# Two mixing tiles become a seven-product pair, and the convolution streams are woven in earlier

## The chip, the cores and the metric

The kernel runs on one core of one Trainium2 chip. The metric is device time in microseconds of one execution; several executions are timed and their median is given. One execution was also profiled.

## The reference

One layer of a hybrid backbone is computed for two groups that share weights: 128 prompt tokens and 512 latent tokens (an 8 x 64 grid), width 1024, all in float32. Both groups are modulated and projected by the same `w_in`:

```python
h = x * (1 + scale) + shift
(v_h, x1, x0, g_h), (q, k, v, g_a), m = split_projection(h, p["w_in"], p["conv_w"], p["conv_b"])
y_h = hyena_long_conv(v_h, x1, x0, h_fwd, h_bwd, p["hyena_d"])   # ((u * filter) + u * d) * x0, u = v_h * x1
y_a = context_attention(q, k, v)              # prompt; latent tokens: neighbourhood_attention
p_h = (y_h * jax.nn.silu(g_h)) @ w_bh
p_a = (y_a * jax.nn.silu(g_a)) @ w_ba
m_h, m_a = jnp.split(jax.nn.sigmoid(m), 2, axis=-1)
out = (m_h * p_h + m_a * p_a) @ w_out
x_new = layer_norm(ALPHA * x + gate * out, p["ln_g"], p["ln_b"])
```

`v_h`, `x1` and `x0` pass a three-tap short convolution first (`split_projection`). The long convolution is done by Fourier transforms. The change concerns the mixing inputs `m` (1024 columns for `m_h`, 1024 for `m_a`) and the order of the work around the convolutions.

## The kernel before

Tokens of both groups stand together, 640 columns, channels on the 128 partitions. Every float32 number that goes into a large matmul is split in a high and a low part, and three products (high x high, high x low, low x high) are added. `hH` and `hL` are the two parts of the modulated input, eight blocks of 128 channels each. The columns of `w_in` are 80 tiles of 128 output channels.

There are two ways to compute projection tiles. `proj` does one tile: 8 blocks x 3 passes x 2 halves of 320 tokens, 48 matmuls of 128x128 by 128x320 (line 182). Its weights come by one load into `raw` on SyncE's queue (SP); ScalarE (ACT) writes the negative low start `wl`, an accumulating load on GpSimd's queue (POOL) adds the weights to it, and ACT writes the high part `wh` (`wtile`, lines 149 to 167). `pair_tile` does two tiles at once by a seven-product scheme on 2 x 2 blocks: seven products of 4 x 3 = 12 matmuls of the same size (line 1239), with sums of weight blocks and sums of token blocks as inputs. The token sums t1 to t4 are made early by `token_sums`, kept in DRAM (`tok_d`) and loaded again by `load_sums`; the weight sums are made by accumulating loads on POOL's queue (`blocks`) and by `sum1` and `sum6` on VectorE (DVE). `high` and `low` split each block sum, ACT the high part, DVE the low.

The program has these stages in order.

1. The prologue: modulation, first tiles, filter input layers.
2. The convolution phase. Its main generator is `quarters()`: per quarter of the channels, `quarter_head` (four short-convolution tiles for u = v_h * x1), `quarter_tail` (two tiles for x0) and a tile group of attention values. Woven into it, as the side generator, is `braid(convs(), filters())`: `long_conv` and `long_conv_back` for each quarter, and `filter_spectrum`, the filters' transforms. `weave(main, side, n_main, n_side)` advances the side n_side steps for each n_main steps of main; `AHEAD_OF` holds the two numbers. The order in which generators issue is a priority; the order on each engine is set from it by a planner when the program is built. `gate_conv(n)` multiplies x0 with the long convolution's output and stores it (`yu_d`), when the second of the two is there.
3. The hand-over (`hand_over`): last x0 tiles, values 0, queries 0, keys 0, then two mixing tiles by `mix_tile`, and the weight loads of the two tiles that follow. When the convolutions are through, `attention_setup` gives their memory to the attention.
4. From here to the end of the attention every engine's order is written out by hand. `first_gates` does two gate tiles by `proj` and prepares the first weight blocks. Then come the heads, eight pairs of attention heads j = 0 to 7, each with its list of pairs from `HEADS`: q makes queries and keys, h and a the branches' gates, m the mixing tiles. A pair counts 14 steps (half-products). The attention of head j (`attend`: scores `tiled`, transposes `turned`) is put between these steps, for j = 0 at the steps listed in line 1407. `later` and `tick` delay work by such steps.
5. The branch projections, the output projection and the norm.

Of the kernel before, what the change touches and what calls it, by code (L numbers as in the profile page):

```python
# [2 lines left out]

# [42 lines left out]
def tile_hyena_natten_step(ctx: ExitStack, tc: tile.TileContext, a, o):  # L46
# [404 lines left out]
        nc.scalar.activation(x[:, 4:10:5], two(pp[:]), AF.Copy)  # L451
        yield

    N_FILTER = 11

    zss = []
    for i in range(2):
# [68 lines left out]
    def quarter_tail(q):  # L526
        for i in range(2):
            n = 2 * q + i
            out["x0"][n] = row(yhp, "yh", f"x0_{n}", n=NG + 1)
            yield from conv_tile(16 + n, out["x0"][n])  # L530
            gate_conv(n)
            yield

    def long_conv(q):
        us, ident = out[f"u{q}"], out["ident"]
# [159 lines left out]

    N_VALUES = 11

    AHEAD_OF = 5, 3

    SUMS = ("t2", "t3", "t1", "t4")  # L700

# [50 lines left out]
    def chain(*gens):  # L752
        for g in gens:
            yield from g
# [4 lines left out]
    head = quarter_head(0)  # L759
    next(head)  # L760
    dft_consts()
    weave(head, filter_spectrum(0), 2 + NK, N_FILTER)
    pinned[0] = False
    sums = chain(token_sums(0), token_sums(1))

    def along(main, side, every):
        for i, _ in enumerate(main):
# [86 lines left out]
    def hand_over():  # L854
        yield from quarter_tail(3)
        hwa_stack.close()
        load_sums(0, SUMS[:2])
        out["slots_l"] = left.enter_context(tc.tile_pool(name="slots_l", bufs=1))
        out["slots_q"] = left.enter_context(tc.tile_pool(name="slots_q", bufs=1))
        first_blocks()  # L860
        yield from chain(values(0), queries(0), keys(0))
        yield from mix_tile(0)
        last_mix = mix_tile(1)
        yield next(last_mix)
        for i in range(2):
            wraw(T_GA + i)
        yield from last_mix
        for i in range(2):
            early[T_GA + i] = wtile(T_GA + i, "dma")
        load_a(0)  # L870

    def mix_tile(n):
        th = row(yhp, "yh", f"mx{n}")
        for hf, p in enumerate((yield from proj(T_MH + n, eng="dma"))):
            nc.scalar.activation(th[:, CS[hf]], p[:, :HALF], AF.Tanh, scale=0.5)
        nc.scalar.dma_start(mh_d[n], th[:])
        yield

    def first_gates():
        yield from gate_a(0)  # L880
# [510 lines left out]
    with tc.manual_schedule(engines=engines):  # L1391
        for _ in first_gates():
            pass
        sums_of_second()
        scratch()
        load_sums(0, SUMS[2:3])
        load_sums(1, SUMS[2:3])
        load_a(1)
        load_sums(0, SUMS[3:])
        load_sums(1, SUMS[3:])  # L1400
        biases[0] = [bias_tile(h) for h in range(2)]
        for j in range(8):
# [12 lines left out]
        drain()  # L1415
# [311 lines left out]
```

## Time and profile before

| | |
|---|---|
| median of three runs | 880.49 us (879.66 to 881.36) |
| the profiled execution | 881.71 us, span 879.9 us |
| TensorE (PE) busy | 867.0 us, 99% |
| VectorE (DVE) busy | 638.6 us, 73% |
| ScalarE (ACT) busy | 450.3 us, 51% |
| GpSimd (POOL) busy | 188.6 us, 21% |
| granted TensorE clock, mean | 0.997 |
| DMA | 169.09 MB, 192 GB/s over the span |

The span runs from the first to the last instruction; the execution's own time is 1.8 us more. In the profile's rows, a line such as L182 is the line of the kernel that issued the instruction, `out<-in` are tiles by name with buffer numbers left out, and an arrow in brackets names what ended the idle time before an instruction. PEld is the weight load of a matmul, which overlaps other matmuls.

### The profile page before, as it was taken

The numbers are of one execution on the slowest core, as the hardware profiler recorded it, in microseconds if no ns is written. First come the engines' busy times: TensorE is split into PE (matmuls) and PEld (weight loads), VectorE is DVE, ScalarE is ACT, GpSimd is POOL, SyncE is SP. The second block draws the span as 40 slices with busy tenths as digits, with TensorE's granted clock in tenths as the row PEclk, the third lists the DMA queues.
The fourth block names the chain that finished last, engine by engine and source line by source line (L and its number), as shares of the span: only waits on it lengthen the run. The fifth ranks groups of instructions, "written<-read, shape, count | busy, mean of one in ns | idle before, by whom it ended". The sixth has DMA issues, their size and how long they took to land.

```text
span 879.9 us, 17136 instructions
## 1 busy us (share of the span) xinstructions
PE 867.0 (99%) x6476; PEld 838.1 (95%) x6476; DVE 638.6 (73%) x1215; ACT 450.3 (51%) x956; POOL 188.6 (21%) x216
## 2 busy tenths in 40 slices
PE   8999999999999999999999999999999999999996
PEld 6899999999999999999999999999999999999885
DVE  4679896786786682588867787777777676666666
ACT  4396654545545535367565656656666622233200
POOL 0012211101101111147453434333453200000000
PEclk9999999999999999999999999999999999999998
DMA  8978876546656696998677668675854596445521
GB/s 311 402 175 232 226 212 150 139 108 169 144 119 146 161 224 143 332 299 230 182 214 187 196 163 251 142 219 162 226 143 113 189 337 206 164 151 187 188 91 53
DMA packets 75246, 169.09 MB, mean 192 GB/s; under 512 B 11003, under 2 KB 28667, under 8 KB 75164
## 3 DMA queue, kind: packets, MB, share of 16 engines
q1 hardware_dynamic: 56204, 123.06, 41.6%
q0 software_dynamic: 13632, 39.33, 23.2%
q10 hardware_dynamic: 5328, 5.61, 1.9%
q8 instruction: 51, 0.84, 0.4%
q14 instruction: 31, 0.25, 0.1%
HBM read 143.32 MB, written 23.99 MB: 190 GB/s over the span
## 4 chain that ended last, share of the span: by engine, by line
PE 96%; DVE 2%; ACT 1%; DMA 1%; issue 0%; POOL 0%; POOLq 0%; DVEq 0%; ACTq 0%
PE mm L182 36%; PE sp L1239 29%; PE out L1537 6%; PE v L661 5%; PE s L1045 2%; PE s L952 2%; PE pt L1036 2%; PE ve L672 1%; PE adaT L252 1%; DMA ra<-wall 1%; PE adaT L269 1%; PE fl L400 1%; PE yb L172 1%; PE yb L170 1%; PE yb L171 1%; PE fl L401 1%
## 5 line engine op out<-in xcount | busy, mean ns | idle before, releaser
L1239 PE MATMUL sp<-t,wb 128*128 128x320 f32 x1008 | 158.9, 311 | 0.0
L1239 PEld LDWEIGHTS sp<-t,wb 128*128 128x128 f32 x1008 | 150.1, 188 | 0.5 <-issue 0.5
L1239 PE MATMUL sp<-hH,wb 128*128 128x320 f32 x500 | 120.9, 313 | 0.0
L1239 PEld LDWEIGHTS sp<-hH,wb 128*128 128x128 f32 x500 | 86.0, 188 | 2.6 <-issue 2.6
L162 POOL DMA_DIRECT2D wl<-wall x34 | 30.4, 894 | 258.3 <-ACT wl L161 230.6
L182 PE MATMUL mm<-hH,wh 128*128 128x320 f32 x336 | 81.7, 313 | 0.7 <-ACT hH L328 0.5
L182 PE MATMUL mm<-hL,wh 128*128 128x320 f32 x336 | 80.8, 311 | 0.0
L182 PE MATMUL mm<-hH,wl 128*128 128x320 f32 x336 | 80.4, 310 | 0.4 <-DVE wl L102 0.4
L1239 PE MATMUL sp<-hL,wb 128*128 128x320 f32 x250 | 77.3, 309 | 0.0
L163 ACT ACTIVATE wh<-raw 128x1024 fp32r<-128x1024 f32 x34 | 36.1, 1062 | 48.8 <-PE mm L182 35.5
L1200 DVE TENSOR_TENSOR wb<-s,wb 128x512 fp32r<-128x512 f32 x63 | 45.0, 715 | 19.1 <-ACT wb L1192 18.9
L182 PEld LDWEIGHTS mm<-hH,wh 128*128 128x128 f32 x336 | 56.9, 188 | 1.9 <-ACT hH L328 0.8
L182 PEld LDWEIGHTS mm<-hH,wl 128*128 128x128 f32 x336 | 57.0, 188 | 1.1 <-DVE wl L102 0.9
L182 PEld LDWEIGHTS mm<-hL,wh 128*128 128x128 f32 x336 | 57.0, 188 | 0.9 <-DVE hL L329 0.5
L1007 POOL TENSOR_SCALAR edge<-edge,sm 128x320 f32<-128x320 f32 x32 | 43.3, 1511 | 61.7 <-DVE sm L1005 53.6
L1192 ACT ACTIVATE wb<-s 128x512 fp32r<-128x512 f32 x63 | 39.7, 631 | 32.0 <-PE sp L1239 20.4
L1007 POOL TENSOR_SCALAR p<-p,sm 128x384 f32<-128x384 f32 x32 | 50.0, 1658 | 24.2 <-DVE sm L1005 10.1
L1239 PEld LDWEIGHTS sp<-hL,wb 128*128 128x128 f32 x250 | 47.1, 188 | 0.0
L1537 PE MATMUL out<-woh,yhs 128*128 128x512 f32 (+1 forms) x176 | 45.8, 374 | 0.0
L1227 DVE TENSOR_TENSOR spare_hHp<-sp,yu 128x320 f32<-128x320 f32 x63 | 30.5, 484 | 18.4 <-PE sp L1239 11.4
L182 PE MATMUL mm<-yhs,wh 128*128 128x320 f32 x224 | 42.2, 310 | 0.0
L101 ACT ACTIVATE wh<-raw 128x1024 fp32r<-128x1024 f32 x15 | 15.8, 1059 | 44.8 <-PE mm L182 32.6
(415 smaller groups left out, 2266.0 us busy)
## 6 DMA issues: line engine op xcount, KB each, us to landing
raw<-wall SPq DMA_DIRECT2D x54, 512.0 KB, 3.8
wl<-wall POOLq DMA_DIRECT2D x34, 512.0 KB, 6.4
ra<-wall SPq DMA_DIRECT2D x21, 512.0 KB, 4.8
rb<-wall SPq DMA_DIRECT2D x40, 256.0 KB, 5.4
ada<-wada SPq DMA_DIRECT2D x16, 512.0 KB, 7.9
tm<-bias SPq DMA_DIRECT2D x16, 512.0 KB, 7.5
s<-wall SPq DMA_DIRECT2D x21, 256.0 KB, 5.0
s<-wall POOLq DMA_DIRECT2D x21, 256.0 KB, 4.3
```

Of the source, the lines that this page charges most:

```text
L162: nc.gpsimd.dma_start(wl, a["wall"][i], accum_op=ALU.add)
L163: nc.scalar.activation(wh, raw[:], AF.Copy)
L182: nc.tensor.matmul(ps[hf][:, :HALF], wt[k], x[:, hf * HALF : (hf + 1) * HALF], start=(i == 0 and k == 0), stop=(i == lead[2] and k == NK - ...
L661: nc.tensor.matmul(ps[t // 2][:, t % 2 * 256 : t % 2 * 256 + 256], x[:, k, P * t : P * t + P], wk, start=first and t % 2 == 0, stop=last, ...
L952: nc.tensor.matmul(dst[h], x[rows(h), qs], y[rows(h), ks], start=i == 0, stop=i == 2, skip_group_check=True)
L1007: nc.gpsimd.tensor_scalar_mul(pv, pv, sm[:, 2, c : c + 1])
L1036: nc.tensor.transpose(pt[:, i * P : i * P + P], ps[h][:, c : c + P], ident)
L1192: nc.scalar.activation(made[g][:, 0], block(g), AF.Copy)
L1200: nc.vector.tensor_tensor(made[g][:, 1], block(g), f(made[g][:, 0]), op=ALU.subtract)
L1227: nc.vector.tensor_tensor(c, dst, c if j == 3 else ps["u"], op=ALU.add)
L1239: nc.tensor.matmul(dst, wk, x(xi, k), start=j < 4 and k == 0 and i == 0, stop=k == 3 and i == 2, skip_group_check=True,)
L1537: ins = nc.tensor.matmul(dst, m[k][:, c0 : c0 + P], w[:, c : c + n], start=(first and k == 0), stop=(last and k == 5), skip_group_check=True,)
```

## The change

The two mixing tiles of the hand-over are taken out and become a pair `m0` at the end of head 0, so head 0 has three pairs and its three attention pieces are placed at steps 14, 24 and 36 instead of 14, 20 and 27. The side generator advances three steps for two main steps instead of three for five. Of the first filter six of eleven steps stay in the first quarter head, and the others are done inside the woven side. `gate_conv` is called for both tiles of a quarter behind the second x0 tile instead of behind each; for the last quarter it is called in the hand-over, behind the loads of the first pair's blocks. The generator `sums` is created later in the text, and runs at the same place.

```diff
-    N_FILTER = 11
+    N_FIRST = 6
...
             yield from conv_tile(16 + n, out["x0"][n])
-            gate_conv(n)
             yield
+        if q < 3:
+            gate_convs(q)
+
+    def gate_convs(q):
+        for i in range(2):
+            gate_conv(2 * q + i)
...
-    AHEAD_OF = 5, 3
+    AHEAD_OF = 2, 3
...
-    weave(head, filter_spectrum(0), 2 + NK, N_FILTER)
+    first_filter = filter_spectrum(0)
+    weave(head, islice(first_filter, N_FIRST), 2 + NK, N_FIRST)
...
         first_blocks()
+        gate_convs(3)
         yield from chain(values(0), queries(0), keys(0))
-        yield from mix_tile(0)
-        last_mix = mix_tile(1)
-        yield next(last_mix)
         for i in range(2):
             wraw(T_GA + i)
-        yield from last_mix
         for i in range(2):
             early[T_GA + i] = wtile(T_GA + i, "dma")
         load_a(0)
-
-    def mix_tile(n):
-        th = row(yhp, "yh", f"mx{n}")
-        for hf, p in enumerate((yield from proj(T_MH + n, eng="dma"))):
-            nc.scalar.activation(th[:, CS[hf]], p[:, :HALF], AF.Tanh, scale=0.5)
-        nc.scalar.dma_start(mh_d[n], th[:])
-        yield
...
-    HEADS = ("q1 h0", "q2 h1 m1", "q3 m2 a2", "q4 h2 m3", "q5 m4 a4", "q6 h3 m5", "q7 a6", "m6 m7")
+    HEADS = ("q1 h0 m0", "q2 h1 m1", "q3 m2 a2", "q4 h2 m3", "q5 m4 a4", "q6 h3 m5", "q7 a6", "m6 m7")
...
     def filters():
-        for q in range(3):
-            yield from chain(until(f"used{q}"), filter_spectrum(q + 1))
-            out[f"spectrum{q + 1}"] = True
-
-    out["spectrum0"] = True
+        for q in range(4):
+            yield from chain(until(f"used{q - 1}"), filter_spectrum(q)) if q else first_filter
+            out[f"spectrum{q}"] = True
...
-                while done in (14, 20, 27) if j == 0 else taken * n_main < done * n_side:
+                while done in (14, 24, 36) if j == 0 else taken * n_main < done * n_side:
```

More of the change, by code (lines that the diff above doesn't have):

```diff
@@ L2 @@
 from contextlib import ExitStack, nullcontext
+from itertools import islice
 import numpy as np
@@ L761, in tile_hyena_natten_step @@
     dft_consts()
-    weave(head, filter_spectrum(0), 2 + NK, N_FILTER)
+    first_filter = filter_spectrum(0)
+    weave(head, islice(first_filter, N_FIRST), 2 + NK, N_FIRST)
     pinned[0] = False
-    sums = chain(token_sums(0), token_sums(1))
     def along(main, side, every):
@@ L1334, in filters @@
     def filters():
-        for q in range(3):
-            yield from chain(until(f"used{q}"), filter_spectrum(q + 1))
-            out[f"spectrum{q + 1}"] = True
-    out["spectrum0"] = True
+        for q in range(4):
+            yield from chain(until(f"used{q - 1}"), filter_spectrum(q)) if q else first_filter
+            out[f"spectrum{q}"] = True
+    sums = chain(token_sums(0), token_sums(1))
     weave(chain(along(quarters(), sums, 2), hand_over()), braid(convs(), filters()), AHEAD_OF[0], AHEAD_OF[1])
```

## The prediction

> **What bounds the kernel now.** I read the page's head first, then the busy shares by stretch, then what TensorE waited for, then the chain of work that ended last.
>
> ```profile
> span 879.9 us, 17136 instructions
> PE 867.0 (99%) x6476; PEld 838.1 (95%) x6476; DVE 638.6 (73%) x1215; ACT 450.3 (51%) x956; POOL 188.6 (21%) x216
> PEclk9999999999999999999999999999999999999998
> ...
> 0.00:50.00 50.00, 47.14 (x483) 40.24 (x484) 30.11 (x60) 22.78 (x41) 1.06 (x14) 1.00 0.85 324
> 50.00:321.00 271.00, 269.95 (x1994) 267.76 (x1993) 207.26 (x308) 153.24 (x293) 40.16 (x54) 1.00 0.70 170
> 321.00:368.00 47.00, 47.00 (x332) 46.99 (x330) 23.17 (x42) 20.56 (x38) 6.79 (x12) 1.00 0.85 217
> 385.00:400.00 15.00, 14.36 (x109) 13.56 (x110) 12.65 (x29) 9.72 (x27) 11.89 (x13) 1.00 0.85 252
> 423.00:469.06 46.06, 46.06 (x364) 44.88 (x362) 35.93 (x88) 28.17 (x72) 20.69 (x20) 1.00 0.70 192
> 816.00:880.00 64.00, 55.60 (x263) 45.80 (x262) 41.13 (x76) 6.39 (x11) 0.93 (x2) 0.96 0.30 107
> ...
> PE s L952 <- ACT pts L1031: 0.6, 1, 0.6
> PE c_X L170 <- ACT uh L101: 0.6, 1, 0.6
> PE c_X L171 <- DVE ul L102: 0.5, 1, 0.5
> ```
>
> In the stretch rows the columns are length, then busy time of PE, weight loads, DVE, ACT and POOL, granted clock, DMA share, GB/s. TensorE is busy in all but 12.9 us of the span. The opening holds 2.86 of that (50.00 less 47.14), the last output tile 8.4 (64.00 less 55.60), and both are outside the change. Between 50 and 816 us there are only two real holes: 1.05 us in the convolution phase and 0.64 us at 385 to 400. DVE, ACT and DMA have spare time in each stretch. So the kernel is a queue of matmuls, and the change is priced first in matmuls, then in holes opened or closed.
>
> What a matmul costs is not its mean duration:
>
> ```profile
> L182 PE MATMUL mm<-hH,wh 128*128 128x320 f32 x336 | 81.7, 313 | 0.7 <-ACT hH L328 0.5 <-ACT wh L101 0.2
> ...
> 352.76 15.55 PE mm L182 x106
> 368.31 12.35 PE sp L1239 x84
> ...
> 701.20 91.57 PE mm L182 x624
> ```
>
> The group says 313 ns for one, but matmuls overlap. The chain's rows give the pace: 91.57 us / 624 = 0.147 us, and 12.35 / 84 = 0.147 us for a whole seven-product pair (7 products x 4 blocks x 3 passes). A pair of ordinary tiles is 2 x 8 x 3 x 2 = 96 such matmuls, 14.1 us.
>
> **The change part by part.**
>
> *The pair.* `mix_tile(0)` and `mix_tile(1)` leave the hand-over and pair `m0` joins `q1 h0`. On TensorE 96 matmuls become 84: 12 x 0.147 = **1.76 us less**. Nothing else on TensorE moves in number. The pair's other work goes beside matmuls:
>
> ```profile
> L1200 DVE TENSOR_TENSOR wb<-s,wb 128x512 fp32r<-128x512 f32 x63 | 45.0, 715 | 19.1 <-ACT wb L1192 18.9
> L1192 ACT ACTIVATE wb<-s 128x512 fp32r<-128x512 f32 x63 | 39.7, 631 | 32.0 <-PE sp L1239 20.4
> L1227 DVE TENSOR_TENSOR spare_hHp<-sp,yu 128x320 f32<-128x320 f32 x63 | 30.5, 484 | 18.4 <-PE sp L1239 11.4
> L1182 DVE TENSOR_TENSOR s<-s,rb x20: 676/682/1002, 374.1 to 672.8; 128x512 f32<-128x512 f32 x20
> L1220 ACT ACTIVATE yu<-sp 128x320 f32<-128x320 f32 x21 | 9.1, 433 | 9.3 <-PE sp L1239 8.4 <-ACT spare_hHp L1278 0.8
> L163 ACT ACTIVATE wh<-raw 128x1024 fp32r<-128x1024 f32 x34 | 36.1, 1062 | 48.8 <-PE mm L182 35.5
> wl<-wall POOLq DMA_DIRECT2D x34, 512.0 KB, 6.4
> ```
>
> DVE gains 7 low halves (7 x 0.715), 6 combinations (6 x 0.484) and two block sums (2 x 0.682): 9.3 us. ACT gains 7 x 0.631 for high halves plus one copy of an accumulator (0.433) and loses four whole-tile copies (4 x 1.062): about +0.6 us; the four tanh and their stores stay (two of 320 KB become four halves on ACT's queue). SP issues four loads (1.28 MB) in place of two (1 MB), POOL two accumulating loads (0.5 MB) in place of two (1 MB). All of it costs nothing while head 0 looks like head 1, which already holds a q, an h and an m pair: in the row 423.00:469.06 TensorE is busy 46.06 of 46.06 us, with DVE at 35.93 and ACT at 28.17. If that cover failed, DVE's 9.3 us would be the most that could come out.
>
> *Head 0's attention pieces.* They ran after half-products 14, 20 and 27 of 28 and now run after 14, 24 and 36 of 42. The third piece is the transposes (`turned(1)`); the next scores (`tiled(2)`) come one half-product into head 1. Before:
>
> ```profile
> 395.65 0.82 PE L1036 MATMUL pt<-pack,p 128*128 128x128 f32 x6
> ...
> 397.92 0.31 PE L1239 MATMUL sp<-hH,wb 128*128 128x320 f32 x1
> 398.81 0.70 PE L952 MATMUL s<-k,q 64*128 64x128 f32 x2 [0.59 <-ACT pts L1031]
> ...
> 397.91 0.47 ACT L1292 ACTIVATE spare_hLp<-spare_hHp 128x320 f32<-128x320 f32 x1 [1.53 <-DVE spare_hHp L1227]
> 398.29 1.61 ACT L1031 ACTIVATE pts<-pt 128x384 f32<-128x384 f32 x4
> ```
>
> Only two half-products (1.76 us) stood between the transposes and the scores that reuse their PSUM banks. ACT, which copies the banks out, sat behind a tanh that waited 1.53 us for DVE. From the last product matmul to the first score is 0.89 us instead of 0.147: 0.74 lost, of which 0.59 is idle. With 36 of 42 there are seven half-products, 6.2 us, and the 1.61 us of copies fit even behind such a tanh. I count **0.74 us less**. The wait could return at another piece; ten steps from 14 to 24 and twelve from 24 to 36 are wider than the six and seven of before, so I do not expect it.
>
> *Streams further in front.* The side generators (filters and long convolutions) advance 3 steps for 2 main steps, where it was 3 for 5; the second half of filter 0 follows inside them. This moves matmuls and DVE work earlier, and adds none. Its price is in holes. Before, the convolution phase lost this:
>
> ```profile
> 168.13 0.38 PE L170 MATMUL c_X<-uh,dftH 128*128 128x256 f32 x1 [0.57 <-ACT uh L101]
> 169.12 0.38 PE L171 MATMUL c_X<-ul,dftH 128*128 128x256 f32 x1 [0.48 <-DVE ul L102]
> ```
>
> TensorE reached the next transform while DVE finished the last one's outputs. That is 1.05 us once in four quarters. The new order could close it (-1.05) or open it in each quarter (4 x 1.05, +3.15 net). DVE is what would do it: 207.26 + 23.17 = 230 us of work in 318, 72%, becomes about 230 in 304, 76%. I take **zero net**, the end that the three quarters without a hole are nearest to, and keep both ends. SP's queue is passed too: each filter's decay loads now stand further ahead of weight loads, and they wait for the buffers that DVE frees:
>
> ```profile
> SPq L63 <- DVE sd L406: 59.8, 15, 7.9
> raw<-wall SPq DMA_DIRECT2D x54, 512.0 KB, 3.8
> ```
>
> The longest such wait was 7.9 us. A weight load behind it has two tiles of matmuls in hand, 14.1 us, for 7.9 + 3.8 and the low half's accumulating load of 6.4: late by 4 us once, if two such waits fell badly; as it did not happen before, zero.
>
> *Gated products.* `gate_conv` moves behind the pair of x0 tiles: the same multiplications and the same eight stores on POOL's queue, some later by one tile (about 7 us, 48 x 0.147). The first reader of `yu_d` is pair h0, after 368 us, so nobody waits. The two weight loads ahead of the gate tiles (`wraw`) no longer stand behind a mix tile on SP; each needs its `raw` buffer from the tile two before it, as ever. Cost nothing; the rotating rows held one tile longer are the way it could show.
>
> *The hand-over.* This is where cover goes: 14.1 us of matmuls between the last key tile and the first gate tile.
>
> ```profile
> L512 DVE TENSOR_TENSOR u<-u,x x8: 817/824/830, 60.7 to 256.1; 128x641 f32<-128x641 f32 x8
> L642 DVE SCALAR_TENSOR_TENSOR u<-u,hyd,y x8: 1140/1156/1179, 163.8 to 353.9; 128x512 f32<-128x512 f32 x8
> 351.29 6.49 SPq L63 DMA_DIRECT2D t<-tok_d  x2
> 362.18 1.34 SPq L63 DMA_DIRECT2D hH<-hHp  x2
> 367.47 2.67 SPq L63 DMA_DIRECT2D t<-tok_d  x4
> t<-tok_d SPq DMA_DIRECT2D x16, 320.0 KB, 6.9
> ```
>
> The last long convolution ended at 353.9, inside the mix tiles, and only then came the memory for the second t3 sum, issued at 351.29 + 6.49 = 357.8. The four quarters of the stream end (353.9 - 163.8) / 3 = 63 us apart. Its last input (the last L512) was there at 256.1, so even at 63 us it could have ended at 319, were it not held behind the earlier quarters. With 2.5 times the steps it should not be. The loads behind it keep their place against the gate tiles: the hH copies at 362.18 wait for the second gate tile to have read hH, and the last t4 load, issued near 370, lands 6.9 later, at about 376.5 to 377, against its first use at 368.31 + 5 x 1.76 = 377.1. That is nearly no slack. After the change the same loads follow the same gate tiles, and the two stores of the mix tiles are gone from that stretch, so I count zero.
>
> Sum: -1.76 - 0.74 = **-2.50 us**. The profiled execution took 881.71 us, 1.8 around its span of 879.9; it would be 879.2. The median of the runs, 880.49, is 1.22 lower, so I predict **878.0 us**.
>
> **The rivals.**
>
> *A, more holes close.* The hole at 168 us goes too: 880.49 - 2.50 - 1.05 = 876.9. For it: filter 0 no longer crowds the start, and scores and transforms are further from their inputs. Against: a denser stream meets its own producers sooner.
>
> *B, holes take the gain.* The hole at 168 appears in each quarter: 878.0 + 3.15 = 881.1, no change to be measured. For it: DVE at 76% and a stream that runs as fast as its dependences. Against: three of four quarters have none. That only the pair's 1.76 comes out (878.7) lies between B and the forecast.
>
> *C, the hand-over stalls (slower).* If the stream ends as late as before while pair 0 starts 14.1 us earlier, the second t3 sum lands at 357.8 + 6.9 = 364.7, and its product would start at 368.31 - 14.1 + 2 x 1.76 = 357.7: TensorE waits 7.0 us, 885.0 in all. It decides the sign from 2.50 us of waiting, and is measurably slower from 4.3 on. For it: SP issues in order, and t1, t4 and the hH copies are queued behind this load. Against: the stream's steps and the 256.1 above. The Trainium skill adds to this one: "TensorE: Matmul & The Clock Gate", section "Why this matters for your kernels", asks for no idle gap over about 3 us, since after one the clock falls to half. The rows here bear it out only at the end, where 8.4 idle us go with a clock of 0.96; the holes of 0.6 us leave it at 1.00. By that rule, with some 3.4 us more at half pace, an estimate from the page, C would be about 1.7 us longer, 886.7; without it, 885.0.
>
> **How the numbers follow.** Forecast 0.40, A 0.23, B and the cases near no change 0.21, C 0.16. The three runs before spread from 879.66 to 881.36, so some 0.2% (1.76 us) is what can be told from no change. The forecast and A lie beyond it on the fast side: faster 0.63; B with the part of the forecast that keeps only the pair: same 0.21; C: slower 0.16. The range runs from A less the run spread of 0.83 and a little (875.7) to B plus 0.87 (882.0); of C most is outside. The forecast's own range is 877.2 to 878.8.
>
> **What would show it.** L182 should lose 96 matmuls, L1239 gain 84, PE busy fall from 867.0 to about 865.3. Head 0 should run as long as head 1, 46 us, with no wait of L952 for L1031. The last L642 should end well before the first gate tile, and the second t3 load be issued right behind the first. In the stretch from 50 us to pair 0 TensorE's idle time should stay near 1 us: less is A, 3 to 4 is B. A PE wait of L1239 for a DMA of t or for `wb`, in the first five products, is C. The prediction is wrong if PE busy does not fall, or if the stretch before pair 0 holds the new waits.

## The result: 11 us slower, the wait is at the first pair

The changed kernel takes 891.46 us (median of four runs, 890.62 to 891.93) against 880.92 for the kernel before (four runs, 879.66 to 882.04): ratio 1.0119, 95% interval 1.0101 to 1.0137. Predicted were 878.0 us, in 875.7 to 882.0. The profiled execution took 891.93 us, with a span of 890.2, 10.3 more than the span of before.

The page's head of the changed kernel:

```profile
span 890.2 us, 17153 instructions
PE 869.6 (98%) x6464; PEld 839.6 (94%) x6464; DVE 646.3 (73%) x1229; ACT 449.7 (51%) x960; POOL 190.0 (21%) x216
PEclk9999999999999999799999999999999999999998
```

TensorE has 12 matmuls fewer and yet 2.6 us more busy time (869.6, before 867.0). The clock row says why: one slice in the middle has a 7, so some matmuls there ran slowly. The stretches around that slice (columns as in the prediction):

```profile
50.00:319.00 269.00, 269.00 (x1991) 267.23 (x1990) 201.55 (x303) 152.41 (x291) 39.74 (x54) 1.00 0.70 172
319.00:352.60 33.60, 33.13 (x235) 32.92 (x233) 20.96 (x34) 11.52 (x24) 1.72 (x2) 1.00 0.48 113
352.60:366.00 13.40, 7.13 (x30) 6.67 (x29) 10.67 (x22) 6.44 (x13) 3.34 (x8) 0.62 0.70 250
366.00:379.70 13.70, 11.07 (x61) 9.89 (x59) 7.30 (x19) 5.02 (x15) 0.00 (x0) 0.88 1.05 361
```

From 50 to 319 us there is no hole at all, and one of 0.47 us follows up to 352.6. Nearly everything is lost from 352.6 to 379.7: TensorE idles 6.27 + 2.63 = 8.9 us, at granted clocks of 0.62 and 0.88. What it waited for, from TensorE's waits:

```profile
PE sp L1235 <- ACT wb L1188: 6.3, 1, 6.3
PE sp L1235 <- DMA t<-tok_d: 2.6, 3, 1.2
```

Both are in the first pair (L1235 is line 1239 of before): its first product waits for the high part of a weight block, later ones for the token sums t. The high part (L1188) is not late by itself. In ScalarE's queue it stands behind the first gate tile's tanh, and that, with the load of its table, waited for the last gated product:

```profile
356.49 1.28 ACT L500 ACT_TABLE_LOAD   x1 [5.01 <-DVE yu L475]
357.78 0.77 ACT L500 ACTIVATE sg<-mm 128x320 f32<-128x320 f32 x2
358.43 0.63 ACT L1188 ACTIVATE wb<-ra 128x512 fp32r<-128x512 f32 x1
```

The chain of work that ended last, around that place (start, length, what):

```profile
354.04 1.02 DVE u L648
355.06 0.67 DVE yu L475 x2
355.75 0.33 SPq L64
...
359.17 6.65 DMA t<-tok_d
365.88 9.56 DMA t<-tok_d
375.49 4.24 PE sp L1235 x17
```

It reads: last long convolution (L648, which was L642), its gated product, the release of memory on which SP's queue stood, loads of t, the pair. SP's queue:

```profile
345.52 11.53 SPq L64 DMA_DIRECT2D t<-tok_d  x4
...
359.17 2.15 SPq L64 DMA_DIRECT2D t<-tok_d  x4
363.66 2.54 SPq L64 DMA_DIRECT2D t<-tok_d  x4
```

The last long convolution on VectorE, before and after:

```profile
353.90 1.18 DVE L642 SCALAR_TENSOR_TENSOR u<-u,hyd,y 128x512 f32<-128x512 f32 x1
```

```profile
353.95 1.11 DVE L648 SCALAR_TENSOR_TENSOR u<-u,hyd,y 128x512 f32<-128x512 f32 x1
```

The stream ended at 355.08 before and ends at 355.06 now. It did not move. Of the four t loads of the first row one left at 345.5, and the next stood until 355.75; so eleven of the sixteen t loads leave after the stream's end. A pair's products come in the order b11, t2, t3, t1, b21, t4, b22; so the sixth needs the last load, and the seventh is the first that needs nothing more. TensorE's rows for the start of the seventh, before and after:

```profile
378.74 0.31 PE L1239 MATMUL sp<-hH,wb 128*128 128x320 f32 x1
```

```profile
376.99 0.47 PE L1235 MATMUL sp<-hH,wb 128*128 128x320 f32 x1
```

14.1 us of matmuls were taken out from in front of it, and it starts only 1.75 us earlier. Behind it stand 879.9 - 378.74 = 501.2 us before and 890.2 - 376.99 = 513.2 now: the work of the new pair (14.1 - 1.76 = 12.3) less the attention's gain, with a rest of the half clock. So the mixing tiles were not work that could be moved for nothing; they filled the time in which the end of the stream became loads. That reading is tested first, then why the stream did not move.

### The profile page after: what moved, and what is told of

Same layout as the page of the kernel before. It is cut to its first block, busy times and chain, and to the rows that moved or that the text cites. A ratio compares the mean times of both kernels' runs of the same rounds, so it can differ in the third digit from the quotient of the medians.

```text
span 890.2 us, 17153 instructions
## 1 busy us (share of the span) xinstructions
PE 869.6 (98%) x6464; PEld 839.6 (94%) x6464; DVE 646.3 (73%) x1229; ACT 449.7 (51%) x960; POOL 190.0 (21%) x216
## 4 chain that ended last, share of the span: by engine, by line
PE 96%; DMA 2%; DVE 1%; ACT 0%; SPq 0%; issue 0%; POOL 0%; POOLq 0%
PE mm L183 34%; PE sp L1235 30%; PE out L1533 6%; PE v L667 5%; PE s L1041 2%; PE s L948 2%; PE pt L1032 2%; DMA t<-tok_d 2%; PE ve L678 1%; PE adaT L253 1%; PE adaT L270 1%; PE yb L173 1%; PE yb L171 1%; PE fl L401 1%; PE yb L172 1%; PE ut L547 1%
## 5 line engine op out<-in xcount | busy, mean ns | idle before, releaser
L1235 PE MATMUL sp<-t,wb 128*128 128x320 f32 x1056 | 168.5, 313 | 2.6 <-DMA t<-tok_d 2.6
L1235 PEld LDWEIGHTS sp<-t,wb 128*128 128x128 f32 x1056 | 158.8, 190 | 4.1 <-DMA t<-tok_d 2.1
L1235 PE MATMUL sp<-hH,wb 128*128 128x320 f32 x524 | 128.1, 316 | 6.3 <-ACT wb L1188 6.3
L1235 PEld LDWEIGHTS sp<-hH,wb 128*128 128x128 f32 x524 | 91.2, 190 | 9.4 <-ACT wb L1188 6.5
L1235 PE MATMUL sp<-hL,wb 128*128 128x320 f32 x262 | 81.7, 312 | 0.0
L183 PE MATMUL mm<-hH,wh 128*128 128x320 f32 x312 | 75.8, 312 | 0.8 <-ACT hH L329 0.6
L183 PE MATMUL mm<-hH,wl 128*128 128x320 f32 x312 | 75.4, 311 | 0.4 <-DVE wl L103 0.4
L183 PE MATMUL mm<-hL,wh 128*128 128x320 f32 x312 | 74.4, 311 | 0.0
L1188 ACT ACTIVATE wb<-s 128x512 fp32r<-128x512 f32 x66 | 41.6, 632 | 39.5 <-PE sp L1235 20.0
L183 PEld LDWEIGHTS mm<-hH,wh 128*128 128x128 f32 x312 | 52.8, 188 | 2.0 <-ACT hH L329 0.8
L183 PEld LDWEIGHTS mm<-hL,wh 128*128 128x128 f32 x312 | 52.7, 188 | 0.7 <-DVE hL L330 0.5
L1235 PEld LDWEIGHTS sp<-hL,wb 128*128 128x128 f32 x262 | 50.0, 191 | 0.0
```

Of the source, the lines that this page charges most:

```text
L183: nc.tensor.matmul(ps[hf][:, :HALF], wt[k], x[:, hf * HALF : (hf + 1) * HALF], start=(i == 0 and k == 0), stop=(i == lead[2] and k == NK - ...
L1188: nc.scalar.activation(made[g][:, 0], block(g), AF.Copy)
L1235: nc.tensor.matmul(dst, wk, x(xi, k), start=j < 4 and k == 0 and i == 0, stop=k == 3 and i == 2, skip_group_check=True,)
```

## The experiments

Each kernel in one table, from its profiled execution and its runs. "Cover" is the matmuls in TensorE's order from the last y transposes (their own 1.1 us included) to pair 0, each at the pace of the traces. "Stream ends" is the end of the last L648 row (under its number in each kernel), "idle" TensorE's idle time from 50 to 352.6 us, "7th" the start of pair 0's seventh product. The ratio is to the kernel before, on the same chip. Span and median can be of different executions: the profiled one of e3 took 887.3 us, its other three 885.1 to 885.5.

| kernel | cover | idle | stream ends | 7th | span | span less 7th | median | ratio (95%) |
|---|---|---|---|---|---|---|---|---|
| before | 16.7 | 1.05 | 355.1 | 378.7 | 879.9 | 501.2 | 880.5 | |
| after | 1.1 | 0.5 | 355.1 | 377.0 | 890.2 | 513.2 | 891.5 | 1.0119 (1.0101-1.0137) |
| e1 after, mixing tiles back | 15.2 | 0.9 | 354.4 | 377.5 | 877.7 | 500.2 | 880.0 | 1.0003 (0.9994-1.0012) |
| e2 before, pair alone | 3.3 | 1.05 | 354.0 | 376.4 | 889.7 | 513.3 | 890.9 | 1.0123 (1.0108-1.0138) |
| e3 six split buffers | 7.6 | 0 | 349.7 | 373.2 | 885.5 | 512.3 | 885.4 | 1.0059 (1.0042-1.0076) |
| e7 four, tiles moved as in e3 | 1.1 | 0.5 | 355.1 | 377.2 | 890.3 | 513.1 | 891.8 | 1.0129 (1.0113-1.0146) |
| e8 gap filled with matmuls | 1.1 | 0.5 | 355.1 | 377.5 | 889.9 | 512.4 | 891.1 | 1.0124 (1.0108-1.0139) |
| e9 sums from step 20 | 34 | 22.4 | 353.0 | 394.1 | 906.4 | 512.3 | 908.0 | 1.0318 (1.0303-1.0334) |
| e10 sums from step 16 | 15.2 | 8.7 | 355.1 | 378.8 | 891.1 | 512.3 | 893.3 | 1.0154 (1.0139-1.0170) |
| e11 as e9, old rate | 3.5 | 4.6 | 360.9 | 383.0 | 895.4 | 512.4 | 897.0 | 1.0189 (1.0172-1.0206) |
| e4 e3, sums on GpSimd | 13.9 | 7.6 | 355.8 | 378.0 | 890.2 | 512.2 | 892.0 | 1.0132 (1.0117-1.0147) |
| e5 e3, half the sums on GpSimd | 14.2 | 6.0 | 350.4 | 372.2 | 884.9 | 512.7 | 888.1 | 1.0086 (1.0071-1.0101) |
| e6 e4, sums from 28 us on | 17.1 | 6.4 | 353.9 | 380.2 | 892.5 | 512.3 | 894.3 | 1.0159 (1.0144-1.0174) |
| e12 e3, sums from step 12 | 16.8 | 4.0 | 345.9 | 369.8 | 882.3 | 512.5 | 885.6 | 1.0060 (1.0038-1.0082) |
| e13 e3, sums from step 20, 1 in 3 | 17.1 | 4.3 | 348.7 | 373.7 | 886.1 | 512.4 | 886.5 | 1.0071 (1.0054-1.0088) |
| e14 e3, no sums | 14.2 | 0 | 342.6 | 364.0 | 876.3 | 512.3 | 878.2 | 0.9980 (0.9971-0.9990) |
| e17 after, no sums | 9.2 | 0 | 345.8 | 369.8 | 882.1 | 512.3 | 884.0 | 1.0047 (1.0032-1.0062) |
| e18 e2, six buffers, no sums | 13.9 | 0 | 342.9 | 364.1 | 877.6 | 513.5 | 878.8 | 0.9981 (0.9972-0.9991) |
| e15 e3, sums by transfers | 14.2 | 11.0 | 359.0 | 381.9 | 895.5 | 513.6 | 897.3 | 1.0192 (1.0178-1.0206) |
| e16 e15, spaced | 13.9 | 7.5 | 354.1 | 376.2 | 888.4 | 512.2 | 890.0 | 1.0111 (1.0094-1.0128) |

Two columns carry it. Every kernel with pair m0 in head 0 has 512.2 to 513.6 us of span behind the seventh product, so its time is decided by when that product starts. And it never starts less than 21.2 us after the stream ends (e18; 21.9 in the changed kernel). Even in e14 and e18, with about 14 us of cover, it comes 1.2 and 1.3 us later than pair 0's first six products at full pace would bring it (6 x 1.76 us), with a wait for t of 0.4 us in front. So some 21 us are what the loads behind the stream's end need in these kernels.

### Lost cover, or the reweave?

The mixing tiles back in the changed kernel:

```diff
+        yield from mix_tile(0)
+        last_mix = mix_tile(1)
+        yield next(last_mix)
...
-    HEADS = ("q1 h0 m0", ...)
+    HEADS = ("q1 h0", ...)
-                while done in (14, 24, 36) ...
+                while done in (14, 20, 27) ...
```

> The changed kernel, with the two mixing tiles back in the hand-over as ordinary tiles and pair m0 taken out (attention pieces at steps 14, 20, 27 again); the reweave (3 side steps for 2, the split first filter, the moved gated products) stays. Theory 'lost cover': the stream still ends at about 353, and what the change lost is the 14.1 us of matmuls that ran meanwhile. With them back the 8.9 us of waiting and the half clock after 352 us go: 880 to 881 us, the hole at 168 us of 1.05 us perhaps gone too (879.5). Rival 'reweave': the denser stream and its loads are what stalls the hand-over, so this kernel keeps the stall: 889 to 893 us.

And the reverse, the pair alone in the kernel before (the same lines the other way round; old weave, whole first filter in front, `gate_conv` in its old place):

> The kernel before, with only the pair: mixing tiles out of the hand-over, m0 in head 0, pieces at 14, 24, 36; the old weave (3 for 5), the whole first filter in front and the gated products behind each x0 tile. Theory 'lost cover': the stream ends at about 353 here too, so the hand-over stalls as after the change: 889.5 to 893 us, with waits of the first seven-product matmuls for the high part of the weight sum near 6 us and for token sums near 2.6 us. Rival 'reweave': without the denser stream there is no stall, and the two gains of 1.76 and 0.74 come out: 878 to 880 us.

Measured 879.99 and 890.92 us. TensorE's waits for the pair alone:

```profile
PE sp L1228 <- ACT wb L1181: 6.2, 2, 4.2
PE sp L1228 <- DMA t<-tok_d: 2.1, 4, 0.7
```

Lost cover holds on both sides, and the reweave falls as a cause: with it and the tiles there is no loss, without it and without the tiles the loss is the same (890.92 and 891.46). The reweave, the split first filter and the moved gated products together cost and bring nothing that can be measured. The stream ends at 354.0 us with the old weave (e2) and at 355.1 with the new one.

### The price of the half clock

Granted clock in the changed kernel, by stretch:

```profile
352.80:354.80 2.00, 0.04 (x1) 0.00 (x0) 2.00 (x4) 0.00 (x0) 0.00 (x0) 1.00 0.00 0
354.80:359.20 4.40, 0.08 (x1) 0.09 (x1) 2.54 (x8) 2.56 (x4) 1.55 (x6) 0.51 0.52 138
359.20:365.20 6.00, 6.00 (x22) 5.78 (x23) 5.30 (x10) 3.68 (x8) 1.00 (x2) 0.50 1.03 403
365.20:375.40 10.20, 7.65 (x47) 6.67 (x45) 5.88 (x14) 3.42 (x9) 0.80 (x1) 1.00 1.06 348
375.40:379.00 3.60, 3.52 (x14) 3.52 (x15) 1.71 (x6) 1.38 (x5) 0.00 (x0) 0.53 1.03 401
```

The clock halves 2.0 us into the gap, and comes back 6.0 us after the matmuls do; three short waits later it halves again. To price it, the gap was filled:

```diff
+        if p == 0:
+            warm, w = aux("warm")[:, :HALF], operand(ORDER[0], 0)
+            for i in range(40):
+                nc.tensor.matmul(warm, w(0, 0)[:, :P], w(0, 1 + i % 3), start=True, stop=True, ...)
```

> The changed kernel with 40 extra matmuls of 128x128 by 128x320 ahead of pair 0's first product, into a PSUM bank that nobody reads (the output is the same): TensorE works 40 x 0.147 = 5.9 us in the 6.3 us in which it waited. Theory 'the half clock is a price of its own on top of the wait': the clock stays full from 353 to 366 us, the first product still starts at about 359, and the first three products run at 0.147 instead of 0.267 us a matmul; of the 2.7 us lost there what the t loads allow comes back: 888.5 to 890 us. Rival 'the products would have waited for t anyway': 891 to 892 us, with the waits for t longer by what the clock gives.

Measured 891.11. The rows, waits first:

```profile
PE sp L1239 <- DMA t<-tok_d: 3.8, 4, 1.8
```

```profile
359.20:365.20 6.00, 5.17 (x30) 4.42 (x30) 5.30 (x11) 3.71 (x9) 1.18 (x2) 1.00 1.03 401
365.20:368.00 2.80, 0.54 (x2) 0.32 (x3) 1.47 (x3) 0.61 (x1) 0.62 (x1) 1.00 1.04 405
368.00:372.00 4.00, 4.00 (x17) 4.00 (x18) 0.49 (x1) 0.05 (x1) 0.00 (x0) 0.57 1.06 265
```

The clock stayed full through the gap, the products ran faster, and then waited longer for t (3.8 us for 2.6). The forecast of 888.5 to 890 was wrong and the rival right: the seventh product starts at 377.5, and at 377.0 without the filling. The half clock was real, but it lay inside the time the loads needed anyway. It is not gone altogether: the last row has a stretch of it behind the new waits for t, so this prices the gap's half clock and not every one.

### What holds the stream: buffers

The high and low halves of the filter transforms and of the inverse transforms share four rotating buffers. Six of them:

```diff
-            sh = hw.tile([P, 2, 256], F32R, tag="shl", bufs=4, ...)
+            sh = hw.tile([P, 2, 256], F32R, tag="shl", bufs=6, ...)
...   (sl, ph, pl the same; room: e and ye/yep live in X and R, arg in another buffer)
```

> The changed kernel with six instead of four rotating buffers for the high and low halves that the filter transforms and the inverse transforms share; the room comes from keeping e and ye/yep inside X and R and arg in another rotating buffer. No arithmetic changes. Theory 'the stream is a chain of quarters held by these buffers': the stream runs closer behind its inputs; in the order of TensorE's instructions the last y transposes move some 6.5 us of matmuls further ahead of pair 0, so about 6 to 7 us of the waiting and most of the half clock go: 880 to 884 us. Rival 'VectorE or the loads of the hand-over alone set it': no change, 889 to 893 us.

> The control of the kernel with six split buffers: e, ye/yep and arg are moved in the same way, and the split buffers stay at four. Theory 'the two more buffers are what moved the stream': 890 to 892.5 us, the same waits for wb and t as after the change. Rival 'the moved tiles did it': 884 to 887 us, as with six.

Measured 885.43 and, for the control, 891.75. The stream ends 5.3 us earlier and the seventh product starts 3.8 us earlier, with no new hole. The gain was a little overestimated (880 to 884 us were expected). The buffers are one part of what holds the stream.

### What holds the stream: the token sums' place

The sums t1 to t4 are 26 operations on VectorE, 0.82 us each (128x640), at about 68 to 119 us in the changed kernel, with 8 copies on ScalarE (not the 16 that the first expectation below counts). They were moved further on, and one step of them is taken at each main step where it was one in two; nothing else was changed, but the third kernel has the weave's old rate too:

```diff
-            if i % every == 0:
+            if i % every == 0 and i >= DELAY:
...
-    weave(chain(along(quarters(), sums, 2), ...
+    weave(chain(along(quarters(), sums, 1), ...
```

> The changed kernel with one thing moved: the token sums (26 operations on VectorE, 16 copies on ScalarE in the convolution phase) begin at step 20 of the quarters and then take one step per main step, where they began at step 0 and took one in two. Buffers, weave and all arithmetic are as after the change. In the order built, the last y transposes stand 34 us of matmuls ahead of pair 0 (1.1 after the change, 16.7 before it). Theory 'the stream was held by the sums on VectorE in the first quarter, and a hand-over whose loads go out early needs no cover': the last convolution ends 30 us ahead of pair 0, no wait for wb or t, the seventh product of pair 0 starts near 363.5 us (377.0 after the change) and 512.5 us of work follow: span 876, time 876.5 to 879 us, faster than both kernels. Rival 'the sums on VectorE only move the hole': TensorE waits 3 us or more for VectorE or ScalarE between 90 and 200 us, 880 to 888 us.

> As the kernel with the sums from step 20, but from step 16. In the order built, the last y transposes stand 15.2 us of matmuls ahead of pair 0. Theory 'what counts is the distance between the last convolution and pair 0': the loads of t need about 22 us from the end of the last convolution to the seventh product, 10.6 us of which are pair 0's own products, so 15.2 us is just enough: 877 to 880 us with waits for t under 1.5 us. Rival 'only the sums' place matters, not the distance': the same time as from step 20, within 0.3 us.

> As the kernel with the sums from step 20, and the side generators at the old rate (3 steps for 5 instead of 3 for 2). In the order built, the last y transposes stand 3.5 us ahead of pair 0. Theory 'the denser weave pays only where the sums are out of its way, and the sums' place only with the denser weave': most of the stall is back, 886.5 to 890 us. Rival 'the rate changes nothing': as with the new rate, 876.5 to 879 us.

Measured 908.0, 893.28 and 897.03: all far off, and on the slow side. TensorE's waits with the sums from step 20, and the stretch that holds them:

```profile
PE mm L183 <- ACT zs L485: 5.2, 1, 5.2
PE fa L171 <- ACT sh L102: 4.4, 1, 4.4
PE fb L171 <- ACT sh L102: 2.6, 1, 2.6
```

```profile
140.00:185.00 45.00, 27.78 (x161) 23.68 (x161) 44.45 (x63) 20.03 (x32) 9.96 (x17) 0.78 0.53 168
```

The built order did put the last y transposes 34 us ahead of pair 0. But from 140 to 185 us VectorE is busy 44.45 of 45 us with the sums and the second quarter together, and TensorE, which keeps its order, waits 17 us there. The stream still ends at 353.0. An order that stands earlier only moves the wait when the work that feeds it is not earlier too. The old rate is better here than the new one by 11 us, so my theory that the denser weave pays once the sums are out of its way falls with it. That it pulls more into a place that is already full fits the idle time of 4.6 us for 22.4, and was not tested further.

Spread more evenly, with six buffers (`DELAY` 12, one step in two; `DELAY` 20, one in three):

> As the kernel with six split buffers, with the token sums (on VectorE) begun at step 12 of the quarters, one step in two as before. In the order built, the last y transposes stand 16.8 us of matmuls ahead of pair 0 (7.6 with six buffers alone, 16.7 before the change). Theory 'VectorE's sums in the first quarter hold the stream': the sums now lie in the gaps of the second quarter, where VectorE is busy 65 to 70%; no holes, the last convolution ends near 341, seventh product of pair 0 near 364.5, 877 to 879.5 us. Rival 'each quarter's own chain of 60 to 70 us holds it': TensorE waits for splits (fa, c_X, p_X) 3 to 9 us in the convolution phase, the last convolution still ends at 348 or later: 883 to 890 us.

> The same with the sums begun at step 20 and one step in three. In the order built: last y transposes 17.1 us ahead of pair 0, the second quarter's pulled 4 us further ahead than with the sums from step 12. Theory 'sums hold the stream': 877 to 879.5 us. Rival 'own chain': holes in the second quarter as with the sums from step 16 (8.6 us): 884 to 893 us.

Measured 885.59 and 886.51. The stream ends earlier (345.9 in the first), but holes of 4.0 and 4.3 us open from 140 to 185 us, where VectorE is again the fullest:

```profile
140.00:185.00 45.00, 40.97 (x276) 39.14 (x275) 42.98 (x66) 25.45 (x46) 10.08 (x16) 0.96 0.67 194
```

The rival's times came true. Its reason, that each quarter's own chain holds the stream, is what the next kernels test.

### What holds the stream: the sums' work

The token sums' arithmetic left out: one sum of each half is made and stored under all four names. These three kernels leave work out and do not compute the layer. It was done in the changed kernel, in the kernel with six buffers, and in the pair alone with the old weave and six buffers:

```diff
+        out["sums"] = split(two(hi), two(lo), a_)[1].ins
+        for name in SUMS:
+            yield
+            for i, x in enumerate((hi, lo)):
+                nc.gpsimd.dma_start(tok_d[4 * SUMS.index(name) + 2 * r + i], f(x))
-        nc.vector.tensor_tensor(b_, part(hH, 0, 0), a_, op=ALU.subtract)
...   (and all that follow)
```

> The changed kernel with four split buffers and without the token sums' arithmetic (one sum of each half is made and stored under all four names; VectorE loses 22 and ScalarE 6 operations; the products that use t take wrong numbers of the same size). In the order built, the last y transposes stand 9.2 us ahead of pair 0 (1.1 after the change, 14.2 with six buffers and no sums). Theory 'both hold the stream, each in part': last convolution near 346, seventh product near 368.5, 881 to 884.5 us. Rival 'the sums are all of it': 878 to 880 us. Rival 'without more buffers nothing moves': 889 to 892 us.

> Leaves out the token sums' arithmetic: one sum of each half is made and stored under all four names, so VectorE loses 22 and ScalarE 6 operations of the convolution phase, and the four products that use t take wrong numbers of the same size; stores and loads stay. Six split buffers. In the order built, the last y transposes stand 14.2 us ahead of pair 0. Theory 'VectorE's sums hold the stream': with 18 us of VectorE's work gone there are no holes, the last convolution ends at 341 to 344, 877.5 to 880.5 us. Rival 'own chain': waits for splits of 3 to 9 us in the convolution phase even without the sums, 883 to 890 us.

> The pair alone (old weave of 3 side steps for 5, whole first filter in front, gated products behind each x0 tile), with six split buffers and without the token sums' arithmetic, which are left out as in the run before it. In the order built, the last y transposes stand 13.9 us ahead of pair 0 (14.2 with the denser weave). Theory 'the weave's rate does nothing, the sums and the buffers are what holds the stream': within 1 us of the same kernel with the denser weave, 877.5 to 880 us. Rival 'the denser weave is needed once the sums are out of its way': 882 to 890 us.

Measured 883.99, 878.24 and 878.80. With six buffers, the stream's end and the seventh product:

```profile
341.42 1.13 DVE L647 SCALAR_TENSOR_TENSOR u<-u,hyd,y 128x512 f32<-128x512 f32 x1
```

```profile
363.95 0.31 PE L1211 MATMUL sp<-hH,wb 128*128 128x320 f32 x1
```

The table closes: four buffers with sums 891.5, six buffers 885.4, no sums 884.0, both 878.2. VectorE's 22 operations (18 us) and the two buffers each bring the stream's end forward, by 9.3 and 5.3 us, and 12.5 together, and only together does the seventh product come nearly at its own time (363.95 us, for 352.18 + 6 x 1.76 = 362.7). No hole is left in the convolution phase, so the quarters' own chain did not open the holes above. Then the kernel is 2.1 us faster than before (0.9980, 0.9971 to 0.9990), which is the gain that the prediction named (2.50) for a kernel whose hand-over does not stall. And in that state the old weave gives the same (878.80): the rate of the weave does nothing here either.

Two things stay open. ScalarE loses 6 copies in these kernels and the rotating rows are used less, so VectorE's share is not measured by itself; for it speaks that e4, below, keeps both, moves only VectorE's part to GpSimd, and has nearly the same cover in its order (13.9 us for 14.2). And TensorE has hardly a hole ahead of 352 us in any of the kernels of the two sections on buffers and on the sums' work, so what the edits move is its built order. Whether the stream could have been put earlier in that order with the buffers and the sums as they are was not tested.

### Trying to place the sums elsewhere

All on GpSimd; the second half only; all, tied in the text to the transform constants, with eight first-filter steps in front (on top of six buffers):

```diff
-            ins = nc.vector.tensor_tensor(a_, part(hH, 0, 1), part(hL, 0, 1), op=ALU.add)
+            ins = nc.gpsimd.tensor_tensor(a_, part(hH, 0, 1), part(hL, 0, 1), op=ALU.add)
...   (all that follow the same)
```

> As the kernel with six split buffers, and the token sums t1 to t4 are made on GpSimd instead of VectorE. The last y transposes then stand 13.9 us of matmuls ahead of pair 0, close to the 16.7 us of the kernel before. Theory 'chain held by buffers and by VectorE's queue': the stall is gone and the gains of 1.76 + 0.74 and the hole of 1.05 remain: 877 to 879.5 us, faster than both kernels. Rival 'GpSimd is slower at it and issues the accumulating weight loads, so the sums are late and weights wait': the wait for t stays or moves, 883 to 891 us.

> As the kernel with six split buffers, with the second half of the token sums (those made after about 90 us) on GpSimd and the first half on VectorE. In the order built, the last y transposes stand 14.2 us of matmuls ahead of pair 0 (13.9 with all sums on GpSimd, 7.6 with none, 16.7 before the change). Theory: the loss of the kernel with all sums on GpSimd was VectorE slowed next to GpSimd at 50 to 65 us (four dftL subtractions 9.7 us for 3.1), ahead of the first filter transform; the later sums hit no such place. No wait of fa, about 1.4 us of waits for t, no half clock: 878 to 880.5 us. Rival 'GpSimd slows VectorE wherever it works': new waits of 2 us or more between 90 and 140 us, 882 to 888 us.

> As the kernel with all token sums on GpSimd, but these start only behind the last dftL subtraction, and eight instead of six steps of the first filter stand in front. In the order built, the last y transposes stand 17.1 us of matmuls ahead of pair 0, as much as before the change (16.7). Theory 'cover and no contention at the dftL subtractions': neither the wait of fa at 64 us nor a wait for t or wb: about 1.76 + 1 us below the time of before, 877.5 to 879.5 us. Rival 'contention further on': VectorE's short-convolution rows at 65 to 100 us are slowed (2.2 to 2.9 us for 0.88 in places), a wait comes there instead: 881 to 887 us.

Measured 892.0, 888.13, 894.34. The hand-over is as good as hoped (waits for t of 1.3, 1.0 and 1.6 us), but new waits of 6.0 to 7.6 us stand in the convolution phase, and in the last of the three also ahead of it, where TensorE is busy only 43.1 of the first 50 us.

The last of the three did not do what was meant. GpSimd's first sum, a subtraction on VectorE beside it, and the constants' subtractions:

```profile
28.36 2.20 POOL L727 TENSOR_TENSOR ts<-hH,hL 128x640 f32<-128x640 f32 x1 [26.84 <-ACT hHp L329]
40.24 3.98 DVE L330 TENSOR_TENSOR hL<-hx,hH 128x640 fp32r<-128x640 f32 x1 [0.52 <-DVE hx L328]
L103 DVE TENSOR_TENSOR dftL<-draw,dftH x4: 806/810/811, 64.8 to 67.1; 128x640 fp32r<-128x640 f32 x4
```

The tie did not hold GpSimd back: the sums begin at 28.4 us, ahead of the constants at 64.8 and earlier than with no tie at all (50.2). So this kernel shows the price of sums beside the prologue, and its theory, sums behind the constants, stays untested. VectorE's rows for the constants with six buffers, and then with the sums on GpSimd beside them:

```profile
56.61 2.29 DVE L103 TENSOR_TENSOR dftL<-draw,dftH 128x640 fp32r<-128x640 f32 x3
```

```profile
56.89 7.07 DVE L103 TENSOR_TENSOR dftL<-draw,dftH 128x640 fp32r<-128x640 f32 x3
```

The three take 7.07 us for 2.29. TensorE's waits that follow, with all the sums on GpSimd:

```profile
PE fa L172 <- DVE sl L103: 3.5, 2, 2.4
PE fa L171 <- ACT sh L102: 3.1, 1, 3.1
```

Last, the additions by accumulating transfers, and the same with ScalarE's copy put behind a later tile:

```diff
+        def add(dst, i, j):
+            for t in (hH, hL):
+                nc.gpsimd.dma_start(dst, part(t, i, j), accum_op=ALU.add)
...
+            with tc.issue_after(marks[-1]):       # the second kernel only
                 nc.scalar.activation(two(hi), t, AF.Copy, scale=sign)
```

> Six split buffers, and the token sums' additions are made by accumulating transfers on GpSimd's queue (16 of 320 KB) with six more copies on ScalarE; VectorE keeps 10 of the 26 operations (two sums and eight low halves). Nothing is left out. In the order built, the last y transposes stand 14.2 us of matmuls ahead of pair 0, as in the run without the sums' arithmetic. Theory 'VectorE's time on the sums holds the stream': the last convolution ends near 342 to 345, no holes or under 1 us in the convolution phase, the seventh product near 364 to 366, 877.5 to 880.5 us. Rival 'the transfers stand ahead of the accumulating weight loads on GpSimd's queue': TensorE waits for wl between 60 and 200 us, 882 to 892 us.

> As the kernel with the sums by transfers, and each high half of t is put behind the activation of a later short-convolution tile (two tiles after the first transfers, one after the others), so that the transfer has landed when ScalarE reaches it. Nothing is left out. In the order built, the last y transposes stand 13.9 us ahead of pair 0. Theory 'VectorE's time on the sums holds the stream': waits of TensorE for sh and zs under 2 us in all, last convolution near 343 to 346, seventh product near 364 to 367, 877.5 to 881 us. Rival 'one tile of 7 us is too short for two transfers of 6 to 7 us in a row, and the weight transfers lie behind them': ScalarE still waits 3 to 6 us at each, 884 to 893 us.

Measured 897.29 and 890.01. In the first, neither theory: the queue that stood was ScalarE's. Its row, and TensorE's longest wait:

```profile
74.67 0.74 ACT L720 ACTIVATE t<-ts 128x640 fp32r<-128x640 f32 x1 [7.75 <-DMA ts<-hL]
```

```profile
PE fb L171 <- ACT sh L102: 5.0, 1, 5.0
```

The high half of t waits 7.75 us for its transfer at the head of ScalarE's queue, with the splits behind it. Spacing takes 7.3 us off, but ScalarE still waits for transfers four times, 22.8 us in all and up to 8.3 at once (the rival had 3 to 6 at each); one tile is too short. No kernel here does all the work and beats the kernel before. Whether a wider spacing would, or sums on GpSimd that really start behind the constants, was not tried; nor was memory for t that does not hang on the stream's end.

## Why the prediction was wrong

*The step that failed* is in the paragraph on the hand-over: "Its last input (the last L512) was there at 256.1, so even at 63 us it could have ended at 319, were it not held behind the earlier quarters. With 2.5 times the steps it should not be." It was wrong that the weave's steps hold the stream: it ends at 354.0 us with the old steps (e2) and at 355.1 with 2.5 times as many. Steps are only priorities; what holds the stream are the split buffers and the work on the token sums (e3, e14, e17), and neither changed. So "I count zero" for the hand-over became the whole result: by the forecast's own terms the seventh product should have come at 378.74 - 14.1 = 364.6 (e14: 363.95, with the hole of 1.05 closed too) and came at 376.99, 12.4 us late.

*The row that should have stopped me* was in the same paragraph: the last t4 load "lands 6.9 later, at about 376.5 to 377, against its first use at ... 377.1. That is nearly no slack." I then let the loads "follow the same gate tiles" to an earlier time, though they follow the end of the stream. With the stream where it was, the 14.1 us of cover were to be paid nearly in full.

*Rival C* had the place, the sign and the mechanism, at 0.16, and 885.0 for 891.5. Its price was mis-sized: it priced the wait for one load (the second t3 sum, 7.0 us), where the last of eleven decides. All of them together with the weight blocks run at a DMA share of 1.03 to 1.06 from 359 us on, and the sixth product waits for the last.

*The clock.* C's sentence on the Trainium skill, "TensorE: Matmul & The Clock Gate", section "Why this matters for your kernels", said that a gap of over about 3 us halves the clock. The trace agrees, though the clock fell 2.0 us into the gap of 6.27: the rows have 0.50, and a matmul takes 0.267 us for 0.147. As a price the rule did not help here: with the gap filled the time fell by 0.35 us, inside the spread of the runs, for the 1.7 us that C added for it.

*The pair* (-1.76): right. PE has 12 matmuls fewer, and with no half clock at the hand-over (e14) TensorE is busy 864.9 us, against 865.3 foretold. DVE's and ACT's extra work stayed hidden, as said.

*The attention pieces* (-0.74): right in kind. No wait of the scores for `pts` is left among the waits. Behind the seventh product the span grew by 512.35 - 501.16 = 11.2 us in e14, where 14.1 - 1.76 - 0.74 = 11.6 were due.

*The streams and the gated products* (zero net): right in the sum; after and e2 differ by 0.5 us, e14 and e18 by 0.6. The rows held longer did show, in the tanh that waits 5.01 us for the last gated product, but e2, with `gate_conv` in its old place, loses as much, and its tanh waits 7.79 us for that product. The hole at 168 us closed, as A had it, and B's holes did not come. It is worth nothing that the medians show: e1 has no such hole in its profile and measures 879.99 against 880.08.

*The range* ended at 882.0 because C was given 0.16 and "most is outside". With the stream's steps taken as unproven, C would have had to hold about as much as the forecast.

## What to carry to other kernels

Before moving work out of a place, ask which event behind it is fixed by another chain, and count all the loads that hang on that event, not the first; if the event does not move, the work was cover and comes back nearly in full (here 12.4 of 14.1 us). The weave's rate was no cause of earlier work here: ask which buffers and which engine's queue hold the stream, and move those. An instruction put early on an engine that keeps its order turns into a wait there when what feeds it is not early too.

## What the runs showed of the hardware

- VectorE's subtraction of 128x640 took 0.76 us in a row of three alone (2.29 us) and 2.36 us (7.07 us) while GpSimd worked on tiles of the same size (1.85 to 2.16 us each then). The Trainium skill, "Perfetto Trace Analysis", section "Optimizing Scalar/DVE Operations", warns that the two share a read port, so that moving work between them might not help. The traces agree as far as the slowing goes (in e6 a subtraction of this size took 3.98 us beside GpSimd and 0.82 later), and none of e4 to e6 is faster than before; that the port is the reason, no run here shows.
- The granted clock fell 2.0 us into a gap, and came back 6.0 us after the matmuls had started again; a further half-clock stretch followed waits of 1.2, 1.0 and 0.4 us between 371.2 and 375.5 us.
- An accumulating transfer of 320 KB from SBUF to SBUF took 6.8 us (hH) and 6.0 us (hL) from issue to landing in the median; the copy behind two in a row held ScalarE's queue for 7.75 us. In the list of DMA issues (KB, median us):

```profile
ts<-hH POOLq DMA_DIRECT2D x7, 320.0 KB, 6.8
ts<-hL POOLq DMA_DIRECT2D x7, 320.0 KB, 6.0
```
